# Value, query, key and output projections of a hybrid mixer in passes of 512 columns

## The chip, the cores and the metric

The kernel runs on one core of a Trainium2 chip. The core has five engines that work side by side and wait for each other by semaphores: PE (TensorE, matrix products; PEld is its weight load), DVE (VectorE), ACT (ScalarE), POOL (GpSimd) and SP (SyncE, which here issues nearly all DMAs). The metric is the device time of one execution in microseconds (us); lower is better. Times of a kernel are given as the median of its runs, and a profile belongs to one execution of its own.

## The reference, cut to what matters

Two layers, each a mixer and then a mixture of experts, over 512 latent tokens and 256 context tokens of width 1024. The second layer gives no context output, so there only what the latents read of the context is computed.

```python
h  = rms_norm(x, norm1_g[l]) * (1.0 + sc1) + sh1      # x: 512 latents; the same for 256 context tokens
p  = h @ w_in[l]                                      # 1024 -> 2304 columns
# columns: A (Au 256, Av 256), B 256, C (q 256, k 256, v 256), D (q 256, k 256, v 256)
ya = chunk_spatial_gating(A)                          # gelu, chunks of 128 tokens
yb = fourier_mix(B)
yc = differential attention of C                      # latents read latents and context
yd = neighbourhood attention of D                     # with a relative-position bias, rpb
y  = rms_norm per head of concat(ya, yb, yc, yd)
x  = x + g1 * (y @ w_out[l])                          # 1024 -> 1024
...
aff = softmax(x2 @ router_w[l])                       # x2: normed and modulated x
gate, idx = top_k(aff per expert, n / 8)              # each of 16 experts picks its tokens
x  = x + g2 * scatter(silu(x2[idx] @ wg) * (x2[idx] @ wu) @ wd * gate)
```

Everything is float32. Modulations (sc1, g1 and so on) come from a projection of the conditioning by ada_w, 24 MB a layer.

## The kernel before, in words

**Matrix products of float32.** A weight and an activation are each split into a high part, which PE takes in its fast float32 format (fp32r), and a low remainder; a product is three matmuls (high by high, high by low, low by high). With 8 pieces of the depth of 1024, one output tile of 128 tokens takes 24 matmuls of 128x128 weights (here the activations) by a moving piece of the weight matrix. For the projections the pass is 256 columns wide (`proj_pair`, line L628, two token tiles to a PSUM bank) or, where the output is wanted with tokens along the columns (Au and B), 512 wide (`proj_T`, L639). In the output projection (`wout_unit`, L1327) a unit is one token tile by 256 columns. The attention's C queries and keys (Cqk) already run 512 columns wide (L697).

**Weights and their split.** `Stream` issues the weights in a fixed list (`ORDER`, then w_out, then the experts) on SP's queue, as far ahead as `st.limit` words per partition allow; a step that needs one that hasn't been issued issues it there. 2048 words are one item of 256 columns (1 MB). Items of w_in have a limit of 4096 words at most, so a third item is issued when one has been released (`st.done`, after the projection's last matmul). `wsplit` (L570, L571) has ACT copy the item as the high part and POOL subtract it from the item, in place, for the low part. `wout_split` does the same for w_out, with DVE for the subtraction (L1257, L1259).

**Order in a layer.** Norm of x and its transposes, beside the Cqk projection; `proj_C` (the values of C, Cv); then `c_attn`, the C attention, with B, Dv and the conditioning's projection (ada, L458) dealt out beside it as fillers; `proj_Au`, `proj_Av`; `mix_A`; `proj_D` (Dq and Dk); `d_attn` with `mix_B` and more of ada; the output projection in `UNITS` (24 units in the first layer, 16 in the second, each followed two units later by `front_unit`: transposes L1348 and router logits L1355 of the finished piece of x); `route` (top-k on DVE, L1407 to L1411); the experts (gate and up L1592 for latents and L1600 for context, down L1667 and L1676). In the first layer latents and context have separate routes. The context's route is written in after its last front unit; its chosen rows are gathered by a DMA of POOL (L1455), scaled (L1481) and fed to expert 0. A scheduler of the program orders the instructions of one weave of steps by costs that it estimates; the order on each engine is fixed when the kernel is built.

## Time and profile before

| | us |
|---|---|
| median of 3 runs | 2005.18 |
| lowest and highest of them | 1999.69, 6309.01 |
| the profiled execution | 2003.24 |
| its span in the profile | 2001.5 |

The profiled execution takes 1.7 us more than its span, and 1.9 us less than the median. In its 2001.5 us PE is busy for 1862.4, DVE for 900.9, ACT for 643.2 and POOL for 229.7. By time, the first layer's mixer runs from 0 to 434 us, its output projection to 520, its routes to 550, its experts to about 1130; the second layer's mixer from there to 1434, its output projection to 1498, its route to 1521, and its experts to the end. A row of the profile names line, engine, operation, output and inputs (buffer numbers left out), and times in us; "busy" of PE includes the tail of each matmul, so how fast a row of matmuls goes is read from many of them together.

### The profile page before, as it was taken

What the parts mean: (1) busy time and instruction counts of PE and PEld (TensorE: products, weight loads), DVE (VectorE), ACT (ScalarE), POOL (GpSimd) and SP (SyncE); (2) the same over time, 40 slices, a digit from 0 to 9 for tenths busy, and PEclk for the clock granted to TensorE, in tenths of its full rate; (3) what the DMA queues carried; (4) which work ended last, traced back from release to release, by engine and by line L of the source; (5) the groups of instructions that cost most, each with busy time, mean ns of one, the idle gap of its engine ahead of it and who ended that gap; (6) DMA issues with size and microseconds to landing.
All of it is one profiled execution on the core that took longest, in us unless ns stands there. A gap on an engine that the chain in (4) does not pass through costs nothing.

```text
span 2001.5 us, 32317 instructions
## 1 busy us (share of the span) xinstructions
PE 1862.4 (93%) x13425; PEld 1083.0 (54%) x13425; DVE 900.9 (45%) x1890; ACT 643.2 (32%) x1372; POOL 229.7 (11%) x188
## 2 busy tenths in 40 slices
PE   5999998989799999999999799998896999999998
PEld 3786787679533333333333387696794444444432
DVE  3758565543633433434434575864433223332332
ACT  3357534542232322322222346644530111111111
POOL 0332033101000000000000044132010000000010
PEclk9999889979899999999999899998897999999999
DMA  9116124632599989999988113425726899999995
GB/s 348 39 53 198 43 93 160 226 137 85 196 404 397 385 332 359 376 343 354 358 345 324 68 60 103 143 93 204 270 93 275 359 421 421 420 421 422 421 421 226
DMA packets 128850, 520.25 MB, mean 260 GB/s; under 512 B 11552, under 2 KB 41152, under 8 KB 80064
## 3 DMA queue, kind: packets, MB, share of 16 engines
q1 hardware_dynamic: 126976, 511.90, 66.5%
q0 software_dynamic: 1728, 6.30, 0.9%
q8 instruction: 105, 1.72, 0.3%
q14 instruction: 41, 0.34, 0.0%
HBM read 509.73 MB, written 8.42 MB: 259 GB/s over the span
## 4 chain that ended last, share of the span: by engine, by line
PE 79%; DVE 7%; DMA 6%; ACT 4%; issue 3%; SPq 1%; POOL 0%; DVEq 0%; ACTq 0%; POOLq 0%
PE banks L1592 34%; PE banks L1600 8%; PE banks L1327 5%; PE banks L628 5%; PE banks L1474 3%; PE banks L639 3%; PE banks L697 3%; PE banks L1727 2%; DMA ar<-in_w_in 2%; PE banks L458 2%; PE banks L1728 1%; DMA ar<-in_ada_w 1%; PE banks L1036 1%; PE banks L934 1%; SPq L1030 1%
## 5 line engine op out<-in xcount | busy, mean ns | idle before, releaser
L1592 PE MATMUL banks<-ar,ar 128*32 128x512 f32 (+1 forms) x4576 | 705.1, 596 | 0.0
L1592 PEld LDWEIGHTS banks<-ar,ar 128*32 128x32 f32 (+1 forms) x4576 | 199.0, 119 | 403.3 <-issue 381.9
L1600 PE MATMUL banks<-ar,ar 128*32 128x512 f32 x1536 | 201.8, 601 | 0.0
L628 PE MATMUL banks<-ar,ar 128*128 128x256 f32 x1344 | 179.3, 290 | 2.2 <-DVE ar L807 1.7
L628 PEld LDWEIGHTS banks<-ar,ar 128*128 128x128 f32 x1344 | 169.9, 196 | 7.9 <-issue 3.2
L1327 PE MATMUL banks<-ar,ar 128*128 128x256 f32 x960 | 139.1, 300 | 2.2 <-ACT ar L1223 1.3
L1327 PEld LDWEIGHTS banks<-ar,ar 128*128 128x128 f32 x960 | 127.3, 203 | 4.1 <-ACT ar L1223 2.4
L408 ACT ACTIVATE ar<-banks 128x512 f32<-128x512 f32 x32 | 19.1, 598 | 309.9 <-PE banks L1592 309.9
L1600 PEld LDWEIGHTS banks<-ar,ar 128*32 128x32 f32 x1536 | 50.3, 111 | 117.1 <-issue 109.5
L1731 DVE TENSOR_TENSOR ar<-ar,banks 128x512 f32<-128x512 f32 x128 | 82.3, 682 | 58.1 <-PE banks L1728 57.8
L1690 DVE SCALAR_TENSOR_TENSOR ar<-banks,gcol,ar 64x512 f32<-64x512 f32 x62 | 46.5, 750 | 118.9 <-PE banks L1592 118.2
L571 POOL TENSOR_TENSOR ar<-ar,ar 128x2048 fp32r<-128x2048 f32 x14 | 64.8, 4628 | 183.8 <-ACT ar L570 143.8
L458 PE MATMUL banks<-ar,S 128*32 128x256 f32 x768 | 62.4, 401 | 21.1 <-DMA ar<-in_ada_w 20.1
L697 PE MATMUL banks<-ar,ar 128*128 128x512 f32 (+1 forms) x288 | 72.7, 399 | 5.9 <-DVE ar L598 3.2
L1479 ACT ACTIVATE ar<-banks,modT,modA 128x128 f32<-128x128 f32 x80 | 30.6, 456 | 142.1 <-PE banks L1474 92.0
L906 ACT ACTIVATE ar<-banks,mx 128x768 f32<-128x768 f32 (+1 forms) x80 | 65.3, 819 | 33.0 <-DVE mx L903 30.5
L903 DVE TENSOR_REDUCE mx<-banks 128x1 f32<-128x768 f32 (+1 forms) x80 | 66.6, 845 | 15.7 <-PE banks L898 12.0
L1474 PEld LDWEIGHTS banks<-ar,ar 128*128 128x128 f32 x512 | 64.2, 202 | 16.4 <-issue 13.0
L1474 PE MATMUL banks<-ar,ar 128*128 128x128 f32 x512 | 68.2, 291 | 2.6 <-DVE ar L1498 2.6
L1481 DVE TENSOR_SCALAR ar<-banks,modA,modT 128x128 f32<-128x128 f32 x80 | 27.4, 403 | 94.6 <-PE banks L1474 61.2
L1669 DVE COPY ar<-banks 128x512 f32<-128x512 f32 x32 | 22.1, 692 | 101.7 <-PE banks L1667 101.7
L1661 DVE TENSOR_TENSOR ar<-banks,ar 64x512 f32<-64x512 f32 x32 | 21.8, 680 | 95.2 <-ACT ar L1606 95.2
(343 smaller groups left out, 2583.4 us busy)
## 6 DMA issues: line engine op xcount, KB each, us to landing
ar<-in_exp_w_gate SPq DMA_DIRECT2D x128, 1024.0 KB
ar<-in_exp_w_up SPq DMA_DIRECT2D x128, 1024.0 KB
ar<-in_exp_w_down SPq DMA_DIRECT2D x124, 1024.0 KB
ar<-in_ada_w SPq DMA_DIRECT2D x96, 512.0 KB
ar<-in_w_in SPq DMA_DIRECT2D x18, 1024.0 KB
ar<-in_w_out SPq DMA_DIRECT2D x8, 1024.0 KB
ar<-in_exp_w_down SPq DMA_DIRECT2D x7, 512.0 KB
ar<-in_rpb SPq DMA_DIRECT2D x8, 384.0 KB
```

What stands on the lines that cost most here:

```text
L458: pe.matmul(B[32 * q:32 * q + 32, 0:n], S[:, k, :], w[:, q * n:(q + 1) * n], start=k == 0, stop=k == 7)
L571: pool.tensor_tensor(lo, raw, hi.v, OP.subtract)
L628: pe.matmul(B[:, tt * 256:(tt + 1) * 256], a.r[:, k, t * 128:(t + 1) * 128], b[:, k, :], start=n == 0, stop=n == 23)
L639: pe.matmul(B[:, 0:n1 - n0], b[:, k, c * 128:(c + 1) * 128], a.r[:, k, n0:n1], start=n == 0, stop=n == 23)
L697: pe.matmul(PS[:, t, s], x.r[:, k, t * 128:(t + 1) * 128], w, start=k == 0 and i == 0, stop=k == 7 and i == 2)
L903: dve.tensor_reduce(mx, s, AX, OP.max, negate=True)
L906: act.activation(e, s, AF.Exp, bias=mx, accum_out=sm)
L1327: pe.matmul(B, a[:, c, t * 128:(t + 1) * 128], b[:, k, :], start=i == 0, stop=i == 23)
L1474: pe.matmul(o, X.v[:, t, tile_of(k)], xg[:, t], start=t == 0, stop=t == 3)
L1592: pe.matmul(B[n * 64 + j:n * 64 + j + p, :], xt[:, k, j:j + p], w[:, k - k0, n * 512:(n + 1) * 512], start=k == 0, stop=k == 7)
L1600: pe.matmul(B[j:j + 32, :], xt[:, k, :], w[:, k - k0, n * 512:(n + 1) * 512], start=k < 2, stop=k > 5)
L1731: dve.tensor_tensor(xs, xs, B, OP.add)
```

## The change

- The values of C and D are one item of 512 columns (CDv, 4096 words, two DMAs of 1 MB), projected before `c_attn` by `proj_CD`, six tiles of 24 matmuls of 512 columns, half of each going to the values of C and half to those of D. Dv is no filler of `c_attn` any more (`TURNS_C`).
- The queries and keys of D are one item (Dqk, 4096 words), projected by `proj_D` in six passes of 512 columns; in the second layer the two context tiles take the keys alone, 256 wide.
- `wsplit` writes to one buffer `hib` of 4096 words in place of two rotating ones of 2048. A 512-column item is split in two steps (pieces 0 to 3 of the depth, then 4 to 7) by ACT and POOL. Au has the one half of `hib`, B and Av the other.
- w_out comes in two items of 512 columns (2 MB each), split in two halves, pieces 4 to 7 first. `UNITS` has 12 and 8 units of 512 columns. `front_unit` does four transposes and four logit matmuls; rows for the gathers go out by 512 columns.
- Limits of the streams: `BESIDE[0]` 26624 to 22528, `SAHEAD[1]` 8192 to 6400, and for one moment, before the second half of the transposes, w_in may have 8192 words.

```diff
-WIN = {"Cqk": 768, "Cv": 1280, "B": 512, "Au": 0, "Av": 256,
-       "Dq": 1536, "Dk": 1792, "Dv": 2048}
+WIN = {"CDv": (1280, 2048), "B": (512,), "Au": (0,), "Av": (256,), "Dqk": (1536, 1792)}
...
-BESIDE = (26624, 30720)
+BESIDE = (22528, 30720)
...
-SAHEAD = (4352, 8192)
+SAHEAD = (4352, 6400)
...
-TURNS_C = ("B4 V3 a18", "B2 V3 a18")
+TURNS_C = ("B4 a18", "B2 a18")
...
-UNITS = ("c0 l0 c1 l1 c2 c3 l2 l3", "l0 l1 l2 l3")
-ORDER = ("Cqk", "Cv", "B", "Dv", "Au", "Av", "Dq", "Dk")
+UNITS = ("c0 l0 c1 l1", "l0 l1")
+ORDER = ("Cqk", "CDv", "B", "Au", "Av", "Dqk")
...
-        src = T["w_in"][l, :, WIN[nm]:WIN[nm] + 256]
-        return [(("win", l, nm), (8, 256),
-                 lambda ap: sp.dma_start(ap, src.rearrange("(k p) f -> p k f", p=128)))]
+        src = T["w_in"][l].rearrange("(k p) f -> p k f", p=128)
+        cs = WIN[nm]
+        return [(("win", l, nm), (8, 256 * len(cs)),
+                 lambda ap: [sp.dma_start(ap[:, :, i * 256:(i + 1) * 256], src[:, :, c:c + 256])
+                             for i, c in enumerate(cs)])]
 
...
-        hir = Rot(ar, (8, 256), 2)
-
-        def wsplit(nm):
+        hib = Buf(ar, (2, 2048))
+        def wsplit(nm, at=0):
             raw = st.get(("win", l, nm))
-            hi = hir()
+            n = 256 * len(WIN[nm])
+            hi = shaped((hib.v if n == 512 else hib.v[:, at:at + 1]).rearrange("p a b -> p (a b)"), (8, n))
+            hr = hi.bitcast(F32R)
             lo = st.split(("win", l, nm))
-            act.activation(hi.r, raw, AF.Copy)
-            pool.tensor_tensor(lo, raw, hi.v, OP.subtract)
-            return hi, lo
+            for k in range(0, 8, 2048 // n):
+                ks = slice(k, k + 2048 // n)
+                act.activation(hr[:, ks], raw[:, ks], AF.Copy)
+                pool.tensor_tensor(lo[:, ks], raw[:, ks], hi[:, ks], OP.subtract)
+            return hr, lo
...
+        def proj_wide(wh, wl, t, a=0):
+            B = bank("pj")
+            n = 0
+            for k in range(8):
+                for x, w in ((HTh, wh), (HTh, wl), (HTl, wh)):
+                    pe.matmul(B[:, a:512], x.r[:, k, t * 128:(t + 1) * 128], w[:, k, a:512],
+                              start=n == 0, stop=n == 23)
+                    n += 1
             return B
...
+        st.first = st.limit = 8192
+        st.pump()
+        st.first, st.limit = None, 4096
...
+        def proj_CD():
+            BF["VD"] = VD = Buf(ar, (6, 256))
+            wh, wl = wsplit("CDv")
+            for t in range(6):
+                B = proj_wide(wh, wl, t)
+                act.activation(VC.v[:, t], B[:, 0:256], AF.Copy)
+                (dve.tensor_copy if t % 2 else lambda o, i: act.activation(o, i, AF.Copy))(VD.v[:, t], B[:, 256:512])
+                if t in (1, 3):
+                    sp.dma_start(vscr[l][(t - 1) * 128:(t + 1) * 128].rearrange("(t p) c -> p t c", p=128),
+                                   VD.v[:, t - 1:t + 1])
+            st.done(("win", l, "CDv"))
+        def proj_D():
+            BF["RD"] = RD = Buf(ar, (6, 2, 256))
+            wh, wl = wsplit("Dqk")
+            for t in range(6):
+                a = 0 if cx or t < 4 else 1
+                g = 8 - 4 * a
+                B = proj_wide(wh, wl, t, 256 * a)[:, 256 * a:512]
+                sq = tmp().v[:, 0:64 * g]
+                act.activation(sq, B, AF.Square)
+                s8 = small(8, "s8")[:, 0:g]
+                dve.tensor_reduce(s8, shaped(sq, (g, 64)), AX, OP.add)
+                rs = rsqrt(s8, g, "dp", 1.0 / 64, 8)
+                qn = tmp().v[:, 0:64 * g]
+                dve.tensor_tensor(shaped(qn, (g, 64)), shaped(B, (g, 64)), bc(rs[:, :, None], [128, g, 64]),
+                                  OP.mult)
+                pool.tensor_tensor(RD.v[:, t, a:2].rearrange("p q (h d) -> p q h d", h=4),
+                                   shaped(qn, (2 - a, 4, 64)), bc(ngn[:, a:2, None], [128, 2 - a, 4, 64]), OP.mult)
+            st.done(("win", l, "Dqk"))
...
-                his.append(Buf(ar, (8, 256)))
-            hi = his[n % 2]
-            act.activation(hi.r, raw, AF.Copy)
+                his.append(Buf(ar, (8, 512)))
+            hi = his[n]
             lo = st.split(("wout", l, n))
-            dve.tensor_tensor(lo, raw, hi.v, OP.subtract)
+            for k in (4, 0):
+                ks = slice(k, k + 4)
+                act.activation(hi.r[:, ks], raw[:, ks], AF.Copy)
+                dve.tensor_tensor(lo[:, ks], raw[:, ks], hi.v[:, ks], OP.subtract)
             wh[n], wl[n] = hi, lo
...
-        tm = Rot(ar, (256,), 4)
-        xq = Rot(ar, (256,), 4)
-        sqr = Rot(ar, (256,), 2)
+        tm = Rot(ar, (512,), 2)
+        xq = Rot(ar, (512,), 3)
+        sqr = Rot(ar, (512,), 1)
...
-            for kk in range(2):
+            for kk in range(4):
                 pe.transpose(tb[:, kk * 128:(kk + 1) * 128], xs[:, tile_of(kk)], ident)
             xt = xq().v
             if t % 2:
-                dve.tensor_copy(xt, tb[:, 0:256])
+                dve.tensor_copy(xt, tb)
             else:
-                act.activation(xt, tb[:, 0:256], AF.Copy)
-            for kk in range(2):
-                pe.matmul(LG[r][:, t_, n], xt[:, kk * 128:(kk + 1) * 128], rwa.v[:, r, 2 * n + kk, :],
-                          start=kk == 0, stop=kk == 1)
+                act.activation(xt, tb, AF.Copy)
+            for kk in range(4):
+                pe.matmul(LG[r][:, t_, n], xt[:, kk * 128:(kk + 1) * 128], rwa.v[:, r, 4 * n + kk, :],
+                          start=kk == 0, stop=kk == 3)
...
-            if n < 3 and n + 1 not in wh and (t, n) in ((1, n), (5, n)):
+            if n < 1 and n + 1 not in wh and (t, n) in ((1, n), (5, n)):
                 wout_split(n + 1)
             with tc.issue_after(mh) if i < 3 else ExitStack():
-                wout_unit(t, n, dve if n == 3 else pool)
+                wout_unit(t, n, dve if n == 1 else pool)
...
-                c = (2, 4) if t > 3 else (2, 3, 4)
-                if n + 1 in c:
-                    rows_out(t // 4, 256 * max([0] + [q for q in c if q <= n]), 256 * (n + 1))
+                rows_out(t // 4, 512 * n, 512 * (n + 1))
```

How the change moves instructions, at three places. In these rows a name such as ar_2226 is a buffer, banks is PSUM, c the constants.

SP's queue in the first layer, from the end of the C attention on. Before: the last pieces of ada_w, then Dq's item, a table of the A mixer (in_sgu), Dk's item, the first item of w_out.

```order
L339 DMA ar_3021<-in_ada_w 128x2x512
L348 DMA ar_2226<-in_w_in 128x8x256
L1080 DMA ar_2465<-in_sgu 128x768
L348 DMA ar_2458<-in_w_in 128x8x256
L353 DMA ar_2727<-in_w_out 128x8x256
```

After, with Dqk's two DMAs in place of Dq's and Dk's, and up to the first piece of rpb:

```order
L340 DMA ar_2726<-in_ada_w 128x2x512
L350 DMA ar_2315<-in_w_in 128x8x256 x2
L1095 DMA ar_2323<-in_sgu 128x768
L1118 DMA ar_2657<-in_dftc 128x256
L356 DMA ar_2647<-in_w_out 128x8x512
L972 DMA ar_2670<-in_rpb 128x768
```

Before, Dq's item was issued when Au's was released and Dk's when Av's was. Dqk's 4096 words fit under the limit of 4096 only when both are released, so both its DMAs wait for Av's last matmuls; the first w_out item is 2 MB where it was 1 MB.

ACT in the first layer's start, beside the Cqk projection (L580 is Cqk's second split, L596 and L597 the modulated transposes). Before:

```order
L596 ACTIVATE ar_207<-banks,modT_73,modA_75 128x256
L570 ACTIVATE ar_198<-ar_655 128x2048
L597 ACTIVATE ar_195<-ar_207 128x256
L580 ACTIVATE ar_199<-ar_134 128x2048
L597 ACTIVATE ar_195<-ar_208 128x512
```

After (L589 is Cqk's second split, L579 the split of a w_in item, L605 and L606 the transposes):

```order
L605 ACTIVATE ar_206<-banks,modT_73,modA_75 128x256
L606 ACTIVATE ar_195<-ar_206 128x256
L589 ACTIVATE ar_198<-ar_134 128x2048
L606 ACTIVATE ar_195<-ar_207 128x512
L606 ACTIVATE ar_195<-ar_205 128x512
L579 ACTIVATE ar_197<-ar_422 128x2048
```

Cqk's split stood behind the split of B's item (L570); now it stands ahead of the first w_in split.

PE at the end of the first layer's routes. Before (L1413 to L1418 are the last steps of the latents' route; L1600 is expert 0's gate and up of the context, four rows of four ahead of this piece; L1471 turns the latents' gathered rows; L1592 is expert 0 of the latents):

```order
L1600 MATMUL banks<-ar_4440,ar_4921 32x512 x4
L1413 MATMUL banks<-c_68,ar_4005 64x64
L1414 MATMUL banks<-c_68,ar_4005 64x64
L1418 MATMUL banks<-ar_4006,ar_4000 128x32 x2
L1600 MATMUL banks<-ar_4763,ar_4921 32x512 x4
L1600 MATMUL banks<-ar_4906,ar_4921 32x512 x4
L1600 MATMUL banks<-ar_4922,ar_4921 32x512 x4
L1600 MATMUL banks<-ar_4924,ar_4921 32x512 x4
L1471 MATMUL banks<-c_68,ar_4043 128x128 x8
L1592 MATMUL banks<-ar_4054,ar_4920 32x512 x8
```

After (L1416 to L1435 are the latents' route, L1488 turns gathered rows, first of the context and then of the latents, L1615 is expert 0 of the context; the latents' L1607 follows when all 32 of L1615 are done):

```order
L1416 MATMUL banks<-c_68,ar_3705 64x128 x2
L1430 MATMUL banks<-c_68,ar_3708 64x64
L1431 MATMUL banks<-c_68,ar_3708 64x64
L1435 MATMUL banks<-ar_3709,ar_3703 128x32 x2
L1488 MATMUL banks<-c_68,ar_3745 128x128 x8
L1615 MATMUL banks<-ar_3958,ar_4277 32x512 x2
L1615 MATMUL banks<-ar_4278,ar_4277 32x512 x2
L1615 MATMUL banks<-ar_3958,ar_4277 32x512 x2
L1615 MATMUL banks<-ar_4278,ar_4277 32x512 x2
L1615 MATMUL banks<-ar_3960,ar_4277 32x512 x2
L1615 MATMUL banks<-ar_4280,ar_4277 32x512 x2
L1488 MATMUL banks<-c_68,ar_3746 128x128 x4
```

The context's expert work, half of which stood ahead of the latents' route on PE and half amid it, now stands behind the whole route; the 32 are the same in number.

## Rows read from the trace of the kernel before

**Rows 1.** The page: busy time by engine, the chain's shares.

```profile
PE 1862.4 (93%) x13425; PEld 1083.0 (54%) x13425; DVE 900.9 (45%) x1890; ACT 643.2 (32%) x1372; POOL 229.7 (11%) x188
...
PE 79%; DVE 7%; DMA 6%; ACT 4%; issue 3%; SPq 1%; POOL 0%; DVEq 0%; ACTq 0%; POOLq 0%
```

**Rows 2.** Groups by line and shape: busy us, mean ns | idle before.

```profile
L628 PE MATMUL banks<-ar,ar 128*128 128x256 f32 x1344 | 179.3, 290 | 2.2 <-DVE ar L807 1.7 <-ACT ar L793 0.4
...
L1327 PE MATMUL banks<-ar,ar 128*128 128x256 f32 x960 | 139.1, 300 | 2.2 <-ACT ar L1223 1.3 <-DVE ar L1330 0.9
```

**Rows 3.** The chain in time, first layer's projections (start us, us, what).

```profile
84.12 15.35 PE banks L628 x128
99.47 5.47 PE banks L639 x24
...
465.25 2.87 PE banks L1327 x24
468.77 2.87 PE banks L1327 x24
```

**Rows 4.** The chain at the first layer's start.

```profile
46.33 6.73 DMA ar<-in_w_in
...
55.36 4.45 issue
59.81 3.38 DVE ar L582
63.23 2.07 PE banks L697 x4
```

**Rows 5.** Timeline of POOL, then of DVE, from 55 us.

```profile
55.07 4.54 POOL L571 TENSOR_TENSOR ar<-ar,ar 128x2048 fp32r<-128x2048 f32 x1 [21.28 <-ACT ar L570]
...
55.32 4.56 DVE L598 TENSOR_TENSOR ar<-ar,ar 128x256 fp32r<-128x256 f32 x1 [1.60 <-ACT ar L597]
```

**Rows 6.** The chain between the two attentions of the first layer.

```profile
241.89 5.41 DMA ar<-in_w_in
...
266.69 5.24 DMA ar<-in_w_in
271.95 1.92 ACT ar L570
...
319.26 6.28 DMA ar<-in_rpb
```

**Rows 7.** Timeline of POOL from 273 us.

```profile
273.95 4.63 POOL L571 TENSOR_TENSOR ar<-ar,ar 128x2048 fp32r<-128x2048 f32 x1 [4.31 <-ACT ar L570]
```

**Rows 8.** L628 in 26 us behind Av's end, each layer (ns min/median/max).

```profile
L628 PE MATMUL banks<-ar,ar x146: 278/283/415, 266.4 to 289.6; 128*128 128x256 f32 x146
...
L628 PE MATMUL banks<-ar,ar x167: 274/283/388, 1320.8 to 1346.9; 128*128 128x256 f32 x167
```

**Rows 9.** Stretches: busy us (count) by engine, granted clock, DMA share, GB/s.

```profile
420.00:434.00 14.00, 9.81 (x53) 7.34 (x51) 8.20 (x22) 4.92 (x10) 0.21 (x1) 0.73 0.29 103
434.00:478.00 44.00, 42.83 (x341) 41.85 (x341) 13.03 (x30) 13.37 (x38) 8.74 (x12) 0.85 0.18 60
...
1600.00:2000.00 400.00, 389.28 (x1874) 168.81 (x1870) 120.67 (x194) 53.29 (x96) 9.36 (x4) 1.00 0.96 398
```

**Rows 10.** Timeline of PE around the first layer's routes.

```profile
518.95 0.72 PE L1327 MATMUL banks<-ar,ar 128*128 128x256 f32 x4
...
529.54 4.99 PE L1600 MATMUL banks<-ar,ar 128*32 128x512 f32 x32
...
542.54 5.30 PE L1600 MATMUL banks<-ar,ar 128*32 128x512 f32 x32
...
550.59 1.92 PE L1592 MATMUL banks<-ar,ar 128*32 128x512 f32 x16
```

**Rows 11.** The chain there: the gathers of context and of latents.

```profile
518.35 4.39 DMA ar<-rows,icoli
...
544.22 4.28 DMA ar<-rows,icoli
```

85 lines of the change are left out of this document (26 added, 59 removed).

## The prediction

> **What bounds the kernel now.** First the page: PE is busy for 1862.4 of 2001.5 us and holds 79% of the chain that ended last [rows 1]. The average hides three kinds of stage, so the stretches come next [rows 9]: in the second layer's experts, from 1600 us on, the DMA engines are 0.96 busy at 398 GB/s, so that stage lasts as long as its weights take and only its start can move; the projections and the output projection are rows of matmuls with nothing between them; and around the hand-overs (420 to 434 us) PE idles and its clock is granted at 0.73. The chain in order of time says which hand-overs count: one at the start [rows 4], two for weights between the attentions [rows 6], the routes [rows 11]. The mean of one matmul (290 and 300 ns for 256 columns [rows 2]) is no price, since it includes the tail that the next one covers; the pace of a row is. The sum is made against the profiled execution's 2003.24 us, 1.9 below the median of 2005.18.
>
> **Pace of the wide passes.** 128 matmuls of 256 columns take 15.35 us, 0.120 each; 24 of 512 columns take 5.47, 0.228 each [rows 3]. A pair so gains 0.012 us. Values of C and D: 288 narrow become 144 wide in each layer, 34.5 against 32.8 us, 1.7 a layer. Dqk: 1.7 in the first layer; in the second, 240 narrow (28.8) become 96 wide and 48 narrow (27.7), 1.1. Output projection: units follow each other by 3.52 us, of which 2.87 are its 24 matmuls [rows 3] and 0.65 transposes and logits, which stay the same in number. 24 units (84.5) become 12 of 5.47 + 1.30 (81.2), a gain of 3.3; in the second layer 16 become 8, 2.2. Together **11.7 us gained**. All of these rows are on the path, so it counts in full. Half the weight loads go too, but they overlap matmuls (PEld is a row of its own [rows 1]); the pace has them in it.
>
> The row shows 0.120 and 0.228 us. The Trainium skill (TensorE: Matmul & The Clock Gate, Back-to-back issue gap) gives 262 and 518 cycles for 256 and 512 columns at 2.4 GHz, which is 6 cycles saved by a pair. By it the 1008 pairs would gain an estimated 2.5 us and not 11.7. The rows are this kernel's own, with fp32r and its weight loads, so the sum goes by them.
>
> **The first layer's start.** ACT stands 6.73 us waiting for B's weights with Cqk's second split queued behind it; then POOL's split of 4.54 us and a DVE subtraction that takes 4.56 beside it run side by side, and only then does DVE split Cqk (3.38), so that PE resumes at 63.23 [rows 4, 5]. In the new order Cqk's split stands first, ahead of any wait for weights, and PE could resume some 6 us earlier. But CDv's split has two POOL steps of that length, which fall beside the DVE work that the attention's start needs and hold it as this one did. Between 0 and 6 us gained; I take **3**, half, since one of two such holds still lies on the path. In the second layer the queue had no such wait on the chain: nothing.
>
> **Dv from beside to before.** It leaves the fillers of the C attention and goes ahead of it, where DVE's norms and rotations of q and k cover part of it. PE has the same work on either side. Nothing, by up to 3 us either way; were the attention short of fillers, ada's matmuls are the next in line.
>
> **Dqk's weights.** This is the largest term. Call the end of Av on PE T. Before, Dq's weights came while Av ran (issued 241.89, 5.41 us to land), and the second wait, for Dk's (266.69, 5.24 us), lay under Dq's matmuls [rows 6]: in the 26 us from Av's end PE did 146 matmuls of the projection in the first layer and 167 in the second [rows 8], 17.5 and 20.0 us of work at 0.120. Now both megabytes are issued at T. They land at about T+8 (5.24 and a second megabyte at 398 GB/s [rows 9], 2.6). ACT copies a half (1.92 [rows 6]), POOL subtracts it (4.63 [rows 7]): T+15. Beside such a POOL step DVE stands still [rows 5], here with the small steps of Av's last norm, so mix A's matmuls, which are ahead of most of Dqk in PE's order, start at about T+17. ACT's second copy waits for POOL's first step; POOL's second step stands behind two products of mix A and ends at about T+26 in the first layer, T+23 in the second, where there are fewer. PE's order has 20 matmuls of Dqk ahead of the first one that needs the second half in the first layer, 33 in the second. So in 26 us PE gets through 20 x 0.228 = 4.6 us of the projection, and in the second layer 46 x 0.228 = 10.5 (33, then 3 us unhindered). Lost: 12.9 and 9.5, **22.4 us** (the pace is counted above). The work is on the path, since `d_attn` begins with it. Bounds: 10 if ada's matmuls, which now come later, fill most of the wait; 37.5 if nothing of the projection runs in that time. I take the count, because the queue's order is fixed.
>
> **The clock.** From 420 to 434 us PE sat idle for 4.2 us, with a granted clock of 0.73; in the next 44 us, 42.83 of them busy, it was 0.85 [rows 9]. Of the levels 1.2 and 2.4 GHz that is 13 us on the lower one, 6.6 us lost. Waits of 12 us in front of Dqk may do the same, between 0 and 6.6 a layer; some of it was paid there before, so I take **2 lost** for both. The Trainium skill (same page, HAM oscillation) warns of just this: a wait for weights between rows of matmuls lets the clock fall, and the next row starts slow.
>
> **rpb behind a larger transfer.** The wait for it is on the first layer's chain (6.28 us [rows 6]); 2 MB of w_out are now in front of it in SP's queue and not 1: 2.6 us at 398 GB/s, 0 to 2.6, **2.5 lost**. In the second layer it isn't on the chain.
>
> **The first layer's routes.** The last matmul of the output projection ends at 519.67. Before, the context's route was over by then (gather at 518.35), the latents' gather was issued at 544.22 [rows 11], and expert 0's gate and up of the context (4.99 and 5.30 us) ran while DVE worked at the latents' route; the latents' first expert matmul came at 550.59 [rows 10], 30.9 after the end. With units of 512 the context's last front unit comes two units of 6.77 us before the end, where it was nine of 3.52 ahead: its route now shares DVE with the last unit and the latents' route. I put the latents' gather at 26 us after the end and its landing at 30.5 (4.28 [rows 11]); turning and scaling to 33; and of the context's 10.3 us, all of which now stands behind the latents' route on PE, 3.9 can run ahead of that landing. So 33 + 6.4 = 39 us, **8 lost**. Between 2 (the context's experts fully under the gather) and 12.
>
> **Small ones.** In the second layer the last unit's product, sum, square, transposes and logits follow on 512 columns and not 256: **1.5 lost**; in the first it is in the 39. Limits of the streams, buffers and the earlier release of w_in: nothing, as expert weights have eight more microseconds to arrive; were they late, a megabyte costs 2.6.
>
> **Sum.** -11.7 - 3 + 22.4 + 2 + 2.5 + 8 + 1.5 = 21.7 us slower: 2024.9 for the profiled execution, 2026 as a median, with half of the 1.9 us. Nearly all of the gain of the wide passes is given back in front of Dqk.
>
> **Rivals.** (1) *The waits are covered.* PE finds other work in front of Dqk and the context's experts run under the gather: the lower bounds, 10 and 2 in place of 22.4 and 8, with the whole 6 us at the start and no clock loss: 2005 - 11.7 - 6 + 10 + 2.5 + 2 + 1.5 = 2003, and down to 1991 if even the 10 vanishes. For it speaks that ada's matmuls are still open there; against, PE's fixed order. (2) *The clock stays low.* Slower than now by over 2%: after each of the two waits half of Dqk's 144 and 96 wide matmuls run on the lower level, (72 + 48) x 0.228 = 27 us more, and the routes cost 12: 2026 - 2 + 27 + 4 = 2055. It decides from 20 us of lost clock on. For it speaks the stretch from 434 us, where one idle of 4 us cost 6.6 [rows 9]; against, that the rows of 24 from 465 us on are at full pace again [rows 3]. (3) *The pace is not there.* The wide passes, in the places where they now stand, gain a fifth of the 11.7 us or so, since the row of 24 [rows 3] was one of the first attention's and not of these: 9 us fewer, 2035. Against it speaks that both rows of it are of the same operands' shapes. The cycles of the Trainium skill's page named above come to about the same time.
>
> **How the numbers follow.** The forecast, 2010 to 2044, has 0.62; the waits covered 0.2; the clock 0.12; the pace 0.06. The range, 2001 to 2047, takes the forecast, the pace, and about half of the other two. About 2% (40 us) is what a measurement here tells from no change: faster than 1965 needs more than the whole gain and has 0.01; slower than 2045 is the clock and the upper end of Dqk's bounds, 0.14; within, 0.85.
>
> **What would show it.** Right: two DMAs of w_in issued at Av's end, 8 us to the ACT copy, PE idle for 10 us or more in front of Dqk in both layers; 24 wide matmuls of the output projection in 5.4 to 5.5 us; the gap from its last matmul to the latents' first expert matmul near 39 us. Wrong: that gap near 31, little idle ahead of Dqk, or a second layer's expert stage that is no longer as long as it was (480 us).

## The result, and the profile of the changed kernel

The changed kernel takes **2032.12 us** (median of 4 runs, 2029.0 to 2032.95); the kernel before took 2002.43 beside it. The ratio is 1.016, with an interval of 1.0132 to 1.0188; it leaves out one disturbed run of the kernel before, of 6309.01 us. That is 30 to 32 us slower (by the medians, by the ratio), where 21.7 were forecast; the time is inside the predicted range (2001 to 2047) and 6 above the predicted 2026. The profiled execution spans 2030.7 us, against 2001.5.

First the page: PE's row, and the groups of the narrow lines' successors (L648 for the projections, L1344 for the output projection; columns as in [rows 1, 2]).

```profile
PE 1861.7 (92%) x12417; PEld 1030.3 (51%) x12417; DVE 900.6 (44%) x1873; ACT 636.3 (31%) x1331; POOL 224.3 (11%) x159
...
L648 PE MATMUL banks<-ar,ar 128*128 128x512 f32 (+1 forms) x576 | 137.5, 394 | 1.4 <-ACT ar L579 1.4
L1344 PE MATMUL banks<-ar,ar 128*128 128x512 f32 x480 | 125.9, 415 | 0.5 <-DVE ar L1347 0.5
```

A thousand matmuls are gone, and PE's busy time has not moved (1862.4 before [rows 1], 1861.7 now), though the span is 29 us longer. So the loss shows as time in which PE is idle (139 us before, 169 now), and what was won per column doesn't show in the busy time; matmuls at the lower clock, seen below, are one reason. Where the time is lost is read by lining up the ends of the same stages in both traces:

| end of ... (us) | before | changed | shift | gained or lost since the row above |
|---|---|---|---|---|
| first layer: queries and keys of C | 84.1 | 79.0 | -5.2 | -5.2 |
| projection Av | 266.7 | 256.3 | -10.4 | -5.2 |
| projection D | 318.3 | 315.5 | -2.8 | +7.6 |
| output projection | 519.7 | 513.2 | -6.5 | -3.7 |
| start of the latents' experts | 550.6 | 549.4 | -1.2 | +5.3 |
| experts | 1121.4 | 1123.4 | +1.9 | +3.1 |
| second layer: queries and keys of C | 1183.8 | 1191.9 | +8.1 | **+6.2** |
| projection Av | 1321.1 | 1327.3 | +6.2 | -1.9 |
| projection D | 1357.8 | 1379.3 | +21.5 | **+15.3** |
| output projection | 1498.1 | 1517.4 | +19.3 | -2.2 |
| start of the experts | 1529.7 | 1552.2 | +22.5 | +3.2 |
| experts | 1977.7 | 2007.2 | +29.5 | **+7.0** |

**Dqk.** PE's idle time in front of its matmuls (timeline of PE, first layer and then second: L1103 is mix A, L648 Dqk):

```profile
266.09 1.97 PE L1103 MATMUL banks<-ar,ar 128*64 128x128 f32 x16 [8.01 <-DMA ar<-in_sgu]
273.66 1.12 PE L1103 MATMUL banks<-ar,ar 128*64 128x128 f32 x8 [4.01 <-DVE ar L856]
...
1334.22 1.97 PE L1103 MATMUL banks<-ar,ar 128*64 128x128 f32 x16 [6.23 <-DVE ar L856]
1337.58 1.65 PE L648 MATMUL banks<-ar,ar 128*128 128x512 f32 x3 [1.38 <-ACT ar L579]
1344.21 1.97 PE L1103 MATMUL banks<-ar,ar 128*64 128x128 f32 x16 [4.99 <-DVE ar L856]
```

That is 12.0 us in the first layer and 12.6 in the second. In the first layer the longer wait ends with the table in_sgu, whose DMA stands behind Dqk's two in SP's queue: mix A, which is ahead of Dqk on PE, waits for that transfer too. The chain of waits in the second layer behind Av's end (start us, us, what) answers to [rows 6]:

```profile
1327.68 7.85 DMA ar<-in_w_in
1335.62 1.91 ACT ar L579
1338.80 3.35 DVE avv L399
1344.21 1.97 PE banks L1103 x16
1346.18 6.97 PE banks L648 x22
```

Timeline of POOL, then of DVE, in the same place (start, us, instruction, idle before it and its releaser), as in [rows 5, 7]:

```profile
1337.60 4.51 POOL L580 TENSOR_TENSOR ar<-ar,ar 128x2048 fp32r<-128x2048 f32 x1 [4.18 <-ACT ar L579]
...
1347.39 4.59 POOL L580 TENSOR_TENSOR ar<-ar,ar 128x2048 fp32r<-128x2048 f32 x1
...
1338.80 3.34 DVE L399 TENSOR_SCALAR avv<-s 128x8 f32<-128x8 f32 x1
```

The two transfers land 7.85 us after their issue (the prediction had 8), and then come ACT's copy, POOL's step, and beside that step a DVE instruction on 8 columns that takes 3.34 us and ends within 0.05 us of that step. The second POOL step ends at 1351.98, 25 us behind Av's end (the prediction had 23). What PE does in the 26 us behind Av's end is the count that answers to [rows 8], first layer and second, followed by the stretch of the second layer (columns as in [rows 9]):

```profile
L648 PE MATMUL banks<-ar,ar x19: 388/628/796, 268.0 to 279.8; 128*128 128x512 f32 x19
...
L648 PE MATMUL banks<-ar,ar x25: 387/398/796, 1337.6 to 1352.8; 128*128 128x512 f32 x25
```

```profile
1327.30:1353.30 26.00, 13.41 (x64) 10.06 (x63) 14.05 (x22) 10.12 (x17) 14.12 (x6) 0.61 0.26 81
256.30:282.30 26.00, 13.48 (x73) 9.91 (x71) 14.88 (x26) 11.09 (x18) 15.04 (x8) 0.67 0.31 96
```

The median of 628 ns against 388 in the first layer is the clock: half of those 19 matmuls ran on the lower level (they follow each other by 0.427 us there, by 0.23 later), behind the idle times of 8.0 and 4.0 us. In the 26 us behind its own Av's end the kernel before had PE busy for 25.50 us at a clock of 1.00 in the second layer, and for 22.98 at 0.93 in the first:

```profile
1321.10:1347.10 26.00, 25.50 (x222) 24.10 (x221) 17.91 (x45) 14.00 (x33) 11.75 (x8) 1.00 0.31 97
266.40:292.40 26.00, 22.98 (x203) 21.77 (x205) 14.34 (x27) 8.66 (x16) 9.13 (x6) 0.93 0.21 67
```

**The second layer's start**, of which the prediction had nothing. Timeline of PE, then of ACT, POOL and DVE:

```profile
1141.46 2.67 PE L614 MATMUL banks<-c,ar 128*128 128x128 f32 x8 [5.58 <-DVE ar L737]
1150.75 1.11 PE L614 MATMUL banks<-c,ar 128*128 128x128 f32 x4 [6.62 <-DVE ar L603]
```

```profile
1132.26 1.91 ACT L579 ACTIVATE ar<-ar 128x2048 fp32r<-128x2048 f32 x1 [0.36 <-issue]
...
1134.25 4.59 POOL L580 TENSOR_TENSOR ar<-ar,ar 128x2048 fp32r<-128x2048 f32 x1 [175.06 <-ACT ar L579]
1143.50 6.46 POOL L580 TENSOR_TENSOR ar<-ar,ar 128x2048 fp32r<-128x2048 f32 x1 [4.66 <-ACT ar L579]
...
1145.51 4.47 DVE L404 TENSOR_TENSOR n14a<-n14y 128x2 f32<-128x2 f32 x1
```

The split of the values' weights (L579, L580) now stands amid the norm of x. A DVE instruction on two columns takes 4.47 us beside POOL's second step (0.15 in the kernel before) and ends 0.02 us after it, and the modulated transposes that PE waits for (L603) stand behind it. POOL's 6.46 us in turn began while DVE was at a subtraction of 2048 columns, which ended 2.1 us later. The Trainium skill (SBUF — State Buffer, SBUF: two separate sides) says that a GpSimd instruction and a DVE instruction with two SBUF inputs, or in a mode that uses two ports, take the port that they share as an exclusive lock: the one that starts first has it for its whole length, and the other is blocked. The trace agrees, with ends that meet here and in front of Dqk. Of the 6.4 us that PE's two idle times have grown by (3.5 and 2.3 before), this hold is the second, 4.3. The first, 2.1, is about ACT's own copy, which stands between the squares of the norm; no run parts the two.

**The first layer's route**, timeline of PE, which answers to [rows 10]:

```profile
512.70 0.48 PE L1344 MATMUL banks<-ar,ar 128*128 128x512 f32 x1
...
534.02 0.31 PE L1430 MATMUL banks<-c,ar 64*64 64x64 f32 x1 [9.66 <-DVE ar L1424]
...
549.43 0.60 PE L1607 MATMUL banks<-ar,ar 128*32 128x512 f32 x2
...
550.70 5.76 PE L1607 MATMUL banks<-ar,ar 128*32 128x512 f32 x51
```

From the last output matmul (513.18) to the latents' first expert matmul it is 36.2 us, where it was 30.9. Seven of the latents' matmuls stand amid the last of the context's; to the row that follows those undisturbed (550.70) it is 37.5, and the expectations below count to there. **The pace**, in the chain of the second layer, which answers to [rows 3]:

```profile
1191.93 14.77 PE banks L648 x65
...
1504.16 5.51 PE banks L1344 x24
```

That is 0.227 us for a matmul of the values' pass, and 0.230 in a unit of the output projection.

**The second layer's experts**, of which the prediction had nothing either, take 454.9 us instead of 448.0. A stretch near that stage's start, and then one of its middle:

```profile
1582.00:1622.00 40.00, 37.71 (x200) 20.26 (x198) 7.13 (x14) 4.63 (x9) 0.00 (x0) 0.96 0.78 294
1622.00:1722.00 100.00, 98.74 (x492) 46.20 (x490) 32.19 (x53) 12.93 (x24) 0.00 (x0) 1.00 1.01 422
```

In the kernel before, the stretch that answers to the first of them:

```profile
1560.00:1600.00 40.00, 40.00 (x204) 16.88 (x202) 9.04 (x15) 4.89 (x10) 0.00 (x0) 1.00 0.86 346
```

Timeline of PE and of DVE at that start, in the changed kernel:

```profile
1569.88 7.09 PE L1607 MATMUL banks<-ar,ar 128*64 128x512 f32 x32 [2.36 <-DVE ar L1670]
...
1594.46 1.80 PE L1491 MATMUL banks<-ar,ar 128*128 128x128 f32 x11 [2.29 <-DVE ar L1515]
...
1579.56 0.49 DVE L1505 TENSOR_SCALAR ar<-ar,icol 128x512 fp32r<-128x512 f32 x1 [1.19 <-PE banks L1607]
```

L1505 makes the mark by which the rows of the next two experts are selected. In the kernel before both marks were made together at 1518.33, right behind the route (timeline of DVE):

```profile
1518.33 0.88 DVE L1488 TENSOR_SCALAR ar<-ar,icol 128x512 fp32r<-128x512 f32 x2
```

Now the second one waits until PE has read a block of an expert's weights: the mark's second buffer is allocated later in the program, as it was before, but now on memory which that block still holds. So the selection isn't there to fill PE's wait for DVE (2.36 us), is waited for itself (2.29), and the buffers of the weights come free later; in the 40 us from 1582 the DMA engines are 0.78 busy, where the kernel before had 0.86. (L1488 and L1505 are the same line of the two kernels.)

### The profile page after: what moved, and what is told of

The parts are those of the page before. It is cut to its first block, busy times and chain, and to the rows that moved or that the text cites. A ratio compares the mean times of both kernels' runs of the same rounds, so it can differ in the third digit from the quotient of the medians.

```text
span 2030.7 us, 30154 instructions
## 1 busy us (share of the span) xinstructions
PE 1861.7 (92%) x12417; PEld 1030.3 (51%) x12417; DVE 900.6 (44%) x1873; ACT 636.3 (31%) x1331; POOL 224.3 (11%) x159
## 4 chain that ended last, share of the span: by engine, by line
PE 53%; DVE 5%; ACT 2%; DMA 2%; issue 1%; POOL 0%; SPq 0%; ACTq 0%; DVEq 0%; POOLq 0%
PE banks L1607 27%; PE banks L1615 5%; PE banks L1491 3%; PE banks L648 2%; PE banks L1344 2%; PE banks L1742 2%; PE banks L717 1%; PE banks L659 1%; PE banks L1743 1%; PE banks L1682 1%; DMA ar<-rows,icoli 1%; DMA ar<-in_w_in 1%; PE banks L637 1%; DVE mx L918 1%; PE banks L462 1%
## 5 line engine op out<-in xcount | busy, mean ns | idle before, releaser
L1607 PE MATMUL banks<-ar,ar 128*32 128x512 f32 (+1 forms) x4576 | 708.3, 596 | 2.8 <-DVE ar L1670 2.4
L1607 PEld LDWEIGHTS banks<-ar,ar 128*32 128x32 f32 (+1 forms) x4576 | 200.6, 119 | 406.6 <-issue 365.6
L1615 PE MATMUL banks<-ar,ar 128*32 128x512 f32 x1536 | 205.7, 595 | 0.6 <-DVE ar L1498 0.6
L648 PE MATMUL banks<-ar,ar 128*128 128x512 f32 (+1 forms) x576 | 137.5, 394 | 1.4 <-ACT ar L579 1.4
L1344 PE MATMUL banks<-ar,ar 128*128 128x512 f32 x480 | 125.9, 415 | 0.5 <-DVE ar L1347 0.5
L648 PEld LDWEIGHTS banks<-ar,ar 128*128 128x128 f32 x576 | 106.3, 194 | 24.2 <-ACT ar L579 1.8
L1615 PEld LDWEIGHTS banks<-ar,ar 128*32 128x32 f32 x1536 | 51.6, 111 | 116.9 <-issue 108.8
L1344 PEld LDWEIGHTS banks<-ar,ar 128*128 128x128 f32 x480 | 92.5, 199 | 21.0 <-DVE ar L1347 1.1
L580 POOL TENSOR_TENSOR ar<-ar,ar 128x2048 fp32r<-128x2048 f32 x14 | 65.7, 4703 | 207.7 <-ACT ar L579 197.8
L1491 PEld LDWEIGHTS banks<-ar,ar 128*128 128x128 f32 x512 | 65.4, 206 | 16.9 <-issue 12.2
L717 PE MATMUL banks<-ar,ar 128*128 128x512 f32 (+1 forms) x288 | 69.7, 389 | 1.1 <-POOL ar L607 0.6
L659 PE MATMUL banks<-ar,ar 128*128 128x512 f32 (+1 forms) x288 | 66.1, 379 | 3.2 <-POOL ar L580 2.6
```

Of the source, the lines that this page charges most:

```text
L580: pool.tensor_tensor(lo[:, ks], raw[:, ks], hi[:, ks], OP.subtract)
L648: pe.matmul(B[:, a:512], x.r[:, k, t * 128:(t + 1) * 128], w[:, k, a:512], start=n == 0, stop=n == 23)
L659: pe.matmul(B[:, 0:n1 - n0], b[:, k, c * 128:(c + 1) * 128], a.r[:, k, n0:n1], start=n == 0, stop=n == 23)
L717: pe.matmul(PS[:, t, s], x.r[:, k, t * 128:(t + 1) * 128], w, start=k == 0 and i == 0, stop=k == 7 and i == 2)
L1344: pe.matmul(B, a[:, c, t * 128:(t + 1) * 128], b[:, k, :], start=i == 0, stop=i == 23)
L1491: pe.matmul(o, X.v[:, t, tile_of(k)], xg[:, t], start=t == 0, stop=t == 3)
```

## The experiments

The theory from the changed kernel's trace: four places make the loss, each independent of the others: Dqk's weights, the first layer's routes, the second layer's split of the values' weights, and (first put down to the wide output projection) the second layer's experts. All times are medians beside runs of the kernel before on the same chip (2001.0 to 2003.7 us). The rows from dqk_early to cdv_late were run on one chip, those from wout_apart to mended on a second, those from mark2 on on a third, so across these groups the ratios are compared and not the times.

| run | us | ratio to before, 95% interval |
|---|---|---|
| changed kernel | 2032.12 | 1.016 [1.0132, 1.0188] |
| dqk_early | 2016.24 | 1.0079 [1.005, 1.0107] |
| d_apart | 2017.27 | 1.0086 [1.0059, 1.0113] |
| units | 2031.99 | 1.0139 [1.0104, 1.0175] |
| cdv_late | 2025.51 | 1.0119 [1.0092, 1.0145] |
| wout_apart | 2024.98 | 1.0104 [1.0079, 1.013] |
| cdv_only | 2008.41 | 1.0022 [1.0005, 1.0038] |
| cdv_only_late | 2005.24 | 1.0016 [0.9998, 1.0035] |
| mended | 2010.07 | 1.0024 [1.0009, 1.004] |
| mark2 | 2026.37 | 1.0145 [1.0109, 1.0182] |
| cdv_only_mark | 2001.97 | 1.0013 [0.9994, 1.0031] |
| mended_mark | 2001.03 | 1.0006 [0.9987, 1.0025] |
| wout_mended | 2006.28 | 1.0037 [1.0013, 1.0062] |

**Dqk's weights issued earlier** (dqk_early), with all of the wide passes kept:

```diff
         setbanks(pj=[0, 1, 2], M=[4, 5], N=[3, 6, 7])
+        st.first = st.limit = 8192
+        st.pump()
+        st.first, st.limit = None, 4096
         run_all(weave(chain(proj_Au(), proj_Av()), first(head_norm(2), PRIO)))
```

> Only the place where Dqk's two megabytes are issued is changed: with the end of C's attention instead of the end of Av. Theory (most of the loss is Dqk's weights: issued at Av's end, landing 8 us later, then two rounds of ACT copy and POOL step): PE's idle time between Av's end and mix A, 12.0 us in the first layer and 12.6 in the second, falls to under 3 in each, D's stage gives back 15 to 20 us of the 23 that it lost, and the kernel takes 2012 to 2018 us instead of 2032. Rival (the wait is the POOL steps beside DVE, wherever they stand): they then hold up Au's and Av's own work, the idle time moves ahead of Av's end, and the time stays at 2026 to 2032.

16 us less, as the theory had it. The waits shrink to 7.0 us in the first layer and 4.3 in the second, less far than to the expected 3: the transfer is hidden, but the splits are not. The order on PE is another one too: 22 of Dqk's matmuls now stand ahead of mix A's first, since the scheduler arranges the weave anew. Timeline of PE in the first layer, and then the two stretches of 19 us, first layer and second:

```profile
260.04 6.75 PE L648 MATMUL banks<-ar,ar 128*128 128x512 f32 x20 [3.84 <-POOL ar L580]
```

```profile
256.00:275.00 19.00, 12.87 (x56) 9.52 (x56) 14.43 (x22) 6.74 (x13) 13.21 (x7) 0.73 0.27 102
1319.00:1338.00 19.00, 14.71 (x70) 11.19 (x70) 13.64 (x24) 14.97 (x22) 9.07 (x3) 0.73 0.31 111
```

PE is busy for 12.87 us of the first stretch, and for 11.54 of the 19 us right behind its own Av's end (252.9), where the changed kernel has 6.48; and for 14.71 in the second against 6.41. But a POOL step is still waited for.

**Dq and Dk apart again** (d_apart), the rest of the change kept:

```diff
-WIN = {..., "Dqk": (1536, 1792)}
+WIN = {..., "Dq": (1536,), "Dk": (1792,)}
...
-            wh, wl = wsplit("Dqk")
+            for qk, nm in enumerate(("Dq", "Dk")):
+                wh, wl = wsplit(nm, 1 - qk)
```

> Of the change, the second attention's queries and keys alone are undone: Dq and Dk again as two items of 256 columns with narrow passes. Theory (Dqk's weights cost 22 us and its wider pace gave 2.8): 2032 - 20 = 2012 us, between 2008 and 2016, with no idle time over 3 us behind Av's end. Rival (the loss is elsewhere, in the second layer's start and the routes, and a later D only took up time in which the output projection's weights would have been waited for): 2026 to 2032.

15 us less, 1 us above the theory's span and far from the rival's; the profiled execution alone took 2011.95. PE is busy again behind Av's end, at the full clock (26 us of each layer; the second stretch starts 6 us ahead of Av's end, and the 26 us right behind that have the same 24.57 and 1.00):

```profile
256.50:282.50 26.00, 22.99 (x209) 20.72 (x212) 18.57 (x36) 12.27 (x26) 11.95 (x8) 1.00 0.17 57
1310.00:1336.00 26.00, 24.57 (x213) 23.18 (x212) 20.21 (x43) 13.01 (x29) 11.60 (x4) 1.00 0.14 42
```

**The context's units first** (units):

```diff
-UNITS = ("c0 l0 c1 l1", "l0 l1")
+UNITS = ("c0 c1 l0 l1", "l0 l1")
...
-            if n < 1 and n + 1 not in wh and (t, n) in ((1, n), (5, n)):
+            if n < 1 and n + 1 not in wh and (t, n) in ((1, n), (4, n)):
```

> Only the order of the output projection's units in the first layer is changed: both units of the context ahead of both of the latents, so that the context's route starts two units of 6.8 us earlier. Theory (the first layer's routes cost 6.6 us because the context's route shares DVE with the latents'): the gap from the last matmul of the output projection to the first latent expert matmul falls from 37.5 to 30 to 33 us and the time by 4 to 7, to 2025 to 2028. Rival (the experts that follow wait for their own weights, so an earlier start is lost there): the gap falls and the time stays within 2 us of 2032.

The gap falls from 36.2 to 32.9 us, so the place of the context's route makes most of the 5.3 lost, as the theory says; the time stays (within some 4 us, by the ratios), and not for the rival's reason. The width of the units isn't all of it: in the five runs that have the narrow output projection again, the gap is 33.2 to 33.6 and not 30.9. In cdv_only, as an example, a megabyte of expert weights is issued 0.5 us ahead of the context's gather (510.74, 511.26), whose rows reach ACT 9.1 us after the issue; in the kernel before that megabyte comes behind it (519.62, 518.35) and it takes 4.4. No run tests this. The second block of the output projection's weights is now needed four units earlier than its transfer and its split allow. Who released PE in L1344 (us, times), in this run:

```profile
  DVE ar L1276: 7.3, 4
  ACT ar L1275: 1.5, 2
```

In the changed kernel neither of these lines is waited for there. One wait took the place of the other.

**The split of the values' weights later, in the second layer** (cdv_late):

```diff
             run_all(qk_first(range(4), turn(0, True)))
+            mk = latest(mybir.EngineType.Activation)
             run_all(qk_first((4, 5), turn(0, False)))
...
-            wh, wl = wsplit("CDv")
+            with tc.issue_after(mk) if l else ExitStack():
+                wh, wl = wsplit("CDv")
```

> Only the split of the values' weights for C and D in the second layer is changed: its ACT copies, and with them the two POOL steps, stand behind the first block of the queries' and keys' turn and no longer amid the norm of x. Theory (POOL's two steps hold DVE during that norm, which cost 6.2 us that the prediction did not have): PE's idle times at the second layer's start (5.6 and 6.6 us) fall to near those of before (3.5 and 2.3), the queries' and keys' end comes 5 to 7 us earlier, and the time is 2025 to 2027. Rival (the start waits for the experts' last products and the norm itself): the idle times stay and the time is 2031 to 2033.

The idle times and the kernel's time are as the theory had them. The two idle times of PE are near those of before (3.49 and 2.30):

```profile
1135.66 2.67 PE L614 MATMUL banks<-c,ar 128*128 128x128 f32 x8 [3.79 <-DVE ar L737]
1140.65 1.12 PE L614 MATMUL banks<-c,ar 128*128 128x128 f32 x4 [2.31 <-DVE ar L603]
...
1160.93 0.98 PE L717 MATMUL banks<-ar,ar 128*128 128x256 f32 x6 [2.36 <-DVE ar L607]
```

The last line is what the move costs in its new place, beside other DVE work. In this profile 3.0 us of the stage are won from the experts' end to the queries' and keys' end, where the theory had 5 to 7; the rest of the 6.6 is not at that place, and the interval touches that of the changed kernel.

**The output projection in blocks of 256 again** (wout_apart): UNITS, the blocks, the buffers and the limits of the weights' streams as in the kernel before.

```diff
-        src = T["w_out"][l, :, n * 512:(n + 1) * 512]
+        src = T["w_out"][l, :, n * 256:(n + 1) * 256]
...
-UNITS = ("c0 l0 c1 l1", "l0 l1")
+UNITS = ("c0 l0 c1 l1 c2 c3 l2 l3", "l0 l1 l2 l3")
```

> Of the change, the output projection alone is undone: four blocks of 256 columns again, with the old limits of the weights' streams. Theory (the wide projection gains 5.9 us by its pace, but the first layer's route then costs 6.6 us, the second's 3.2, and the second layer's experts take 455 us instead of 448, because their weights come later): 2032 - 11 = 2021 us, between 2017 and 2025, with the second layer's experts at 448 us again. Rival (the longer experts' stage follows from D's late weights, and the wide projection is worth its pace): the experts stay at 454 to 455 us and the time is 2030 to 2038.

The time is the theory's, but one of its reasons fell: the second layer's experts still take 454.6 us. So the wide output projection isn't what made them longer.

**The values' pass alone** (cdv_only): the edits of d_apart and wout_apart together, so that only CDv is left of the change.

> Of the change, only the values of C and D together in one wide pass remain; Dqk and the output projection are undone. Theory (the first layer's start and the pace give 10 us up to Av's end, the second layer's start takes 6): between 1996 and 2002 us, beside 2002 of the kernel before. Rival (a Dv that is moved out of C's attention costs that attention its fillers, so that the gain up to Av's end comes from elsewhere): slower than before by 4 us or more, 2006 to 2012.

The rival's time, but not by its mechanism. The D projection of the first layer ends 6.8 us before that of the kernel before, so the first layer's attention lost no cover that counts; the experts of the second layer take 454.6 us here too, 6.6 more than before. That stage's cause had to come with the values' pass itself, and led to the mark's buffer shown above.

**The same with the later split** (cdv_only_late), by the edit of cdv_late:

> As the last, and in the second layer the split of the values' weights for C and D stands behind the first block of the queries' and keys' turn. Theory (it took 6.6 us from the changed kernel, of which its profile shows 3 at that place): 3 to 6 us below the run that keeps the values' pass alone, 1992 to 1998, so faster than before by 4 to 10. Rival (in the second layer an earlier start is lost again before the experts, whose stage lasts as long as its weights): the same as that run within 2 us.

3 us less than cdv_only, with intervals that overlap; neither the theory's 1992 to 1998 nor a clear nothing. In the profile the queries and keys of the second layer end 8.8 us earlier, but 7.5 of that is there before the edit's place (at the end of the first layer's experts, after the same instructions in the same order), and 1.4 is the edit's. The stretch from D's end to the end of the output projection takes 142.7 us instead of 137.3. The scheduler arranged it anew: PE's and DVE's instructions there stand in another order. cdv_only_mark below, which has the order of this run, takes 142.6 there, so a move in one place can cost in another by the order that the scheduler then finds.

**All wide passes, both waits mended** (mended): the edits of dqk_early and cdv_late.

> All of the wide passes are kept, with two of the waits taken away: Dqk's megabytes are issued with the end of C's attention, and the second layer's split of the values' weights stands later. Theory (the two gains of 16 and 6.6 us add, since they are in different stages): 2009 to 2012 us, still above the 2002 of before by the routes and the second layer's experts. Rival (the second layer's experts wait for their weights, so that the gains in that layer do not add): 2014 to 2017.

As expected: the two gains add (16 + 6.6 of the changed kernel's 2032), as far as times from two chips can tell.

**Two buffers for the marks** (mark2), on the changed kernel:

```diff
-            ohm = Rot(ar, (512,), 1)
+            ohm = Rot(ar, (512,), 2)
...
-                    for r in (xtr, ohm, et, ht):
+                    for r in (xtr, et, ht):
                         r.grow()
```

> The changed kernel with one buffer more: the second layer's marks for the selection of experts' rows have two buffers from the start, and the rotation isn't grown later. Theory (the grown buffer lies on memory that a block of weights holds, so that the second selection comes 40 us later, PE waits twice for 2.3 us and weights follow later): the second layer's experts take 447 to 449 us instead of 455, without those two waits, and the kernel 2024 to 2027 us. Rival (that stage lasts as long as its weights take from the DMA engines, however PE starts): the waits go and the stage stays at 454 to 455 us, the kernel at 2030 to 2033.

The experts of the second layer take 447.9 us, as before, in place of 454.9. Timeline of DVE and of PE, and then the stretch that answers to the one from 1582 us above:

```profile
1538.92 0.88 DVE L1505 TENSOR_SCALAR ar<-ar,icol 128x512 fp32r<-128x512 f32 x2
...
1570.70 7.09 PE L1607 MATMUL banks<-ar,ar 128*64 128x512 f32 x32
```

```profile
1580.60:1620.60 40.00, 40.00 (x204) 16.86 (x202) 9.46 (x16) 6.89 (x13) 0.00 (x0) 1.00 0.91 370
```

Both marks are made at once, the 32 matmuls that stood behind 2.36 us of idle time stand behind none, and the DMA engines are 0.91 busy instead of 0.78. The whole kernel takes 2026.4, as the theory had it; but in the whole kernels' times the 7 us aren't resolved. By the ratios this edit gives 3 us here, and 0.6 and 3.6 in cdv_only_mark and mended_mark below, with intervals that overlap each time.

**The mark's buffers in the three other versions** (cdv_only_mark, mended_mark, wout_mended: the edit of mark2 on cdv_only_late, on mended, and on wout_apart with the edits of dqk_early and cdv_late).

> Of the change only the values' pass of C and D, with the later split in the second layer and two buffers for the marks. Theory (7 us less of the second layer's experts): 1997 to 2000 us, faster than before by 3 to 7. Rival (that stage stays as long as it was): 2004 to 2006.

> All wide passes, Dqk's weights issued with the end of C's attention, the later split in the second layer and two buffers for the marks. Theory (each wait that was found gives its part): 2010 - 7 = 2003 us, between 2000 and 2006, the same as before within what can be told. Rival (the stage of the second layer's experts stays): 2008 to 2012.

> Values' pass and Dqk wide, the output projection in blocks of 256 columns as before, and the three waits taken away (Dqk's weights earlier, the later split, two buffers for the marks). Theory (the wide output projection costs 7 us net, so it adds to the run that keeps all passes): 1995 to 1999 us, faster than before by 4 to 8. Rival (with Dqk early, the projection's gain is kept and its cost was a part of D's wait): 2003 to 2008, no better than the run that keeps all passes.

The second layer's experts take 447.85 to 447.92 us in the three. mended_mark is as expected: with every wide pass kept and the three waits taken away, the time is that of the kernel before (1.0006, interval 0.9987 to 1.0025). cdv_only_mark is 2 us above its theory, and can't be told from before either. In wout_mended the theory fell, and its time is the rival's: the narrow output projection is 5 us worse here, where it was 7 better in wout_apart (6 and 11 by the ratios). From D's end to the first expert matmul the seven profiles with wide units (units itself left out) take 227.7 to 235.9 us in the first layer and 167.9 to 178.4 in the second; the five with narrow ones (the kernel before left out) 229.6 to 236.4, and 167.8 to 176.5. The means are 232.0 and 232.0, 171.8 and 172.5, and the spread within each is far larger, so the net worth of the wide output projection is within some 7 us of nothing, and its sign stays open. No version is faster than the kernel before.

## Why the prediction was right, and where its sum was off

The forecast held: slower by about one and a half per cent, with the largest loss in front of Dqk. By its own steps, forecast against the shifts in the table:

- **Pace of the wide passes**: 0.228 us forecast for 512 columns, 0.227 and 0.230 measured. By the cycles of the Trainium skill (TensorE: Matmul & The Clock Gate, Back-to-back issue gap) the gain would have been an estimated fifth; the rows decide, and the rival that rested on it falls.
- **The first layer's start**: 3 gained, 5.2 measured. The mechanism was right (Cqk's split ahead of any wait): PE's idle time between 40 and 85 us fell from 5.7 to 2.9 us, about the 3 of the forecast. The rest came with the clock, which the sum left out here: the granted clock of these 45 us rose from 0.92 to 1.00.
- **Dv moved**: nothing forecast; the way to Av's end gave 3.5 us beyond its pace in the first layer and 0.2 in the second, so the size was off by up to 3.5, about the bound.
- **Dqk's weights**: the mechanism is shown step by step, and undoing it (d_apart) or hiding its transfer (dqk_early) gives 15 and 16 us back. With pace and clock the forecast for the D stages was 12.2 and 9.4; they measure 7.6 and 15.3, so 21.6 against 22.9 in sum. The first layer's 7.6 is too low: 48 matmuls of ada, which stood amid D's before, now stand right behind its end and take 2.8 us (315.40), so for the same work the shift is 10.4, and the next row of the table gained 6.5. Going by the kernels' times, the way of the weights cost some 18 us (the 15 of d_apart and the 2.8 of pace that it gives up). The count of Dqk's matmuls in the 26 us behind Av's end was forecast as 20 in the first layer (19 measured) and 46 in the second (25 measured). There the error is: the 33 were counted as if they ran from the first half's split on. All but 3 of them stand behind mix A's second step, which started 17 us behind Av's end and took 2.0 (the forecast had mix A's start there; its first step came at 6.9); and those 3 and the next nine ran on the clock's lower level, 0.43 us each. 21 matmuls fewer are 21 x 0.228 = 4.8 us. In the first layer the count is right, but the wait for in_sgu is no part of the forecast's way.
- **The clock**: 2 us forecast. It is seen (0.67 and 0.61 in those 26 us against 0.93 and 1.00), and 10 and 12 of Dqk's matmuls at 0.43 us instead of 0.23 are an estimated 4.4 us; but no run separates it from the waits in front of it; it comes and goes with them (1.00 in d_apart). The rival in which it decided everything falls: behind the stall, from 1346 to 1380 us, it is 0.94.
- **rpb and the output projection**: 2.5 - 3.3 in the first layer, measured -3.7, or -6.5 without ada's 48; 2.2 gained in the second, measured 2.2. The loss behind rpb isn't seen: the first transposes of D's attention (L974, now L989) start 8.5 us behind D's end in both kernels. The experiments can't resolve the net of the whole projection.
- **The first layer's routes**: 39 us forecast for the gap, 36.2 measured (37.5 to the undisturbed row); the latents' gather 26 us after the last matmul forecast, 24.9 measured. units shows the context's route as the cause of most of it, and that a bare reordering pays the same sum elsewhere; about half of the loss stays with narrow units.
- **Limits, buffers, small ones: nothing, and 1.5**: here the sum was wrong. Two terms were missing. The second layer's start cost 6.2 us: the prediction took the first layer's hold of DVE by POOL into account, and wrote "nothing" for the second since no wait for weights stood on its chain; but the new order has the split of the values' weights amid the norm, on ACT and on POOL beside DVE. And a buffer moved onto memory that a weight block holds: 7.0 us in the second layer's experts, which mark2 gives back whole in that stage (447.9). The second layer's route took 3.2 where 1.5 was forecast. With that, one of the prediction's own signs of being wrong came true: from the end of the output projection to that of the experts the second layer takes 489.7 us and not 479.5 (its 480).

The missing 13 us were partly set off by larger gains in the first layer, before Av's end (10.4 where 4.7 was forecast) and between D's end and the output projection's (2.9 more), so the loss came to 29.5 us instead of 21.7 between the profiled executions. That the median is only 6 us above the forecast is in part luck: errors of both signs met, and the kernel before, 2005.18 when the forecast was made, takes 2.8 us less beside the changed one. The rival in which the waits are covered is wrong as a forecast. mended_mark's 2001 us lie inside its 1991 to 2003, but not by its mechanism: PE found no other work there, three waits were taken away by edits, and two of them neither the forecast nor the rival had.

## What to carry to other kernels

Before two weight blocks are merged for a wider pass, follow the larger block's way from issue to split: when its memory comes free, when both halves land, and on which queue and beside which engine's small steps the split runs; here that way cost more than the pace gained, and issuing earlier gave 16 us of it back. After any change of buffers, look in stages that the change doesn't touch for an instruction whose releaser is a reader of other data: one buffer of 2 KB a partition on a held block cost 7 us in the second layer's experts. Ask also where the split of a block falls in the new order: the values' weights were split amid the norm, and POOL's step held DVE.

## What the runs showed of the hardware that was not expected

- A DVE instruction on two columns took 4.47 us beside a POOL subtraction of 2048 columns, and the POOL one itself took 6.46 us, where it takes 4.5 to 4.6 elsewhere; in dqk_early one took 6.26. The DVE instruction and the POOL one ended within 0.02 us of each other.
- In the middle of the second layer's experts the DMA engines of the one core moved 421 to 422 GB/s for 300 us on end, whatever had gone before; the changed kernel and the kernel before differ in the stage's first 70 us (294 against 346 GB/s in the last 40 of them).
- The same instructions in the same order on PE and DVE, from D's end to the end of the output projection in the first layer, took 194.9, 198.3 and 192.1 us in three profiles (dqk_early, mended, mended_mark). A term of a few us can't be read from one profile of that stretch.
